# A hybrid Conformer/Hyena block: the second half of the out-projection in a written order

## The chip, the core and the metric

The kernel runs on one core of a Trainium2 chip. The core has TensorE (PE in the profile: matmuls, whose weight loads, PEld, run beside them), VectorE (DVE), ScalarE (ACT), GpSimd (POOL) and SyncE (SP). Each takes its instructions in order from a queue of its own and waits on semaphores for the others. The queues of SP, POOL and ScalarE also issue transfers to 16 shared DMA engines. The metric is the device time of one execution in microseconds: 2048.83 in the median of three runs of the kernel before (2046.94 to 2049.76).

## What is computed

One encoder layer over 2048 positions and 1024 channels, all in float32: a norm, one input projection to 7168 columns, a Conformer branch (GLU, depthwise convolution of width 31, group norm, swish) and a Hyena branch (short convolution, a long convolution by FFT, group RMS norm), each gated, then one output projection, the residual and a last norm. What matters here is the end:

```python
y = bidir_fftconv(v * x1, h_fwd, h_bwd, hy_skip[l]) * x0
y = group_rmsnorm(y, hy_norm_g[l], N_GROUPS_HYENA) * jax.nn.silu(hy_z)
mix = jnp.concatenate([a, y], axis=-1)
h = h + jnp.einsum('blm,md->bld', mix, w_out[l])
return rmsnorm(h, final_g)
```

## The kernel before

The output projection is made in two halves of 1024 rows of `w_out`. The first half, for the Conformer branch, is spread through the FFT as filler (`conf_steps`) and stored to DRAM as `PT`. The second half, for the Hyena branch, is the last stage and the subject here: 16 blocks of 128 positions. To keep float32 precision each operand is split in a high and a low part, so that one product takes three matmuls (`outproj`, L784 to L786). A block has two column halves of 512, each with 8 chunks of k: 16 parts of three matmuls.

A block's operand is made by these steps, whose names are used throughout:

- **Y, T** (`inverted`): the last stage of the inverse FFT (matmul Y from `v`, a tile named long), copies y on ScalarE, transposes T on TensorE, `m<-T,x` on VectorE (times x0), squares sq on ScalarE.
- **gate, m*gate, vp**: gate is SiLU of `hz` on ScalarE, `m<-m,gate` multiplies it in on VectorE, vp is the mean of the squares by TensorE.
- **r, rs** (`deviations`, `stacked`): root on ScalarE, the long reciprocal on VectorE (128x256), two copies on ScalarE, and rs on VectorE.
- **R, m<-R, mh, ml** (`normed`): two pairs of matmuls spread rs over the partitions into R, of which there is one buffer; `m<-m,R` scales m; mh (ScalarE) and ml (VectorE) are the split.

Then (`residual`, `after`) the row of `PT` and the row of x are loaded by POOL and added ("whole", `row<-row,xr`); after each column half VectorE adds the product (`row<-o,row`, the "half add"; two tiles o) and ScalarE squares it with a sum (sqo, ss); behind the second half come sum, root, reciprocal and the scaling of the row (`row<-row,ss,fg`), and SP stores it. SiLU and root lie in different tables of ScalarE, each loaded by an ACT_TABLE_LOAD.

Up to the last parts of the first half the order on TensorE, SP, ScalarE and VectorE is as written (`tc.manual_schedule`). For the 16 blocks themselves it is not: the loop at the end gives, for each b, the steps of block b+2 and then the parts of block b, and the scheduler of the framework puts the instructions of each engine in an order of its own:

```python
*_, (m, vp) = inverted(b + 2, *(rest[2] if b == 0 else fetched(b + 2)))
st[b + 2] = normed(b + 2, m, deviations(vp))
pts[b + 2] = residual(b + 2)
after(b, pts.pop(b), *st.pop(b))
```

Of the kernel before, what the change touches and what calls it, by code (L numbers as in the profile page):

```python
# [11 lines left out]
F32 = mybir.dt.float32  # L12
# [6 lines left out]
P = 128  # L19
# [162 lines left out]
def hybrid_kernel(ctx: ExitStack, tc: tile.TileContext, A, out):  # L182
# [620 lines left out]
    def conf_steps():  # L803


        state[0] = first.pop()
        raw = mixed_load(1, mix[1])
        for i in range(NB):
            parts = state.pop(i)
            pt = row()  # L810
            for group in [(0,), (1,)] if i + 1 < NB else [(0, 1)]:
                if group == (1,):
                    state[i + 1] = mixed(raw, mix[(i + 1) % 2])
                    if i + 2 < NB:
                        raw = mixed_load(i + 2, mix[i % 2])
                o = {c: out_tile() for c in group}
                for k in range(KT):
                    for c in group:
                        outproj(o[c], 0, *parts, HALF[c], k)
                        held[0] += 1  # L820
                        if k + 1 < KT:
                            yield
                for c in group:
                    nc.vector.tensor_copy(pt[:, HALF[c]], o[c])
                    if c == 1:
                        (nc.sync if i < NB - 2 else nc.gpsimd).dma_start(PT[i * P:(i + 1) * P], pt)
                    yield

    conf = conf_steps()
# [107 lines left out]
    with ExitStack() as c0:  # L937
        ep = c0.enter_context(tc.tile_pool(name="ep", bufs=2, reuse_waits="tile"))
        ps = c0.enter_context(tc.tile_pool(name="psE", bufs=1, space=PSUM, reuse_waits="tile"))
        late = []  # L940

        def rows(x, b, cs=slice(0, D)):
# [15 lines left out]
        def opened(hz):  # L958

            gate = ep.tile([P, NG, P], F32, name="gate", bufs=1)  # L960
            nc.scalar.activation(gate, hz, AF.Silu)
            return gate

        def inverted(b, x0, hz, v, gate=None):

            m = ep.tile([P, NG, P], F32, name="m", bufs=3)
            y, sqs = [], []
            for c in range(2):
                Y = ps.tile([P, TC], F32, name="Y", bufs=2)
                for j in range(2):  # L970
                    mm(Y[64 * j:64 * (j + 1)], winv, v[:, j, HALF[c]], start=True, stop=True)  # L971
                y.append(ep.tile([P, TC], F32, name="y"))
                nc.scalar.activation(y[c], Y, AF.Copy)
            yield
            for c in range(2):
                T = ps.tile([P, 4, P], F32, name="T", bufs=2)
                for k in range(4):
                    nc.tensor.transpose(T[:, k], y[c][:, k * P:(k + 1) * P], ident)
                ks = slice(4 * c, 4 * c + 4)
                nc.vector.tensor_mul(m[:, ks], T, x0[:, ks])  # L980
                sq = ep.tile([P, 4, P], F32, name="sq")
                nc.scalar.activation(sq, m[:, ks], AF.Square)
                sqs += [sq[:, :2], sq[:, 2:]]
                yield
            vp = ps.tile([P, 2 * P], F32, name="vp")
            for g, sq in enumerate(sqs):
                mm(vp[32 * g:32 * (g + 1)], ones_g[:, :32], sq, start=True, stop=True)
            nc.vector.tensor_mul(m, m, gate or opened(hz))
            yield m, vp

        def deviations(vp):
            r = ep.tile([P, 2 * P], F32, name="r")
            nc.scalar.activation(r, vp, AF.Sqrt, bias=epst[:, 0:1])
            nc.vector.reciprocal(r, r)
            return r

        def normed(b, m, r):
            rs = ep.tile([P, 2 * P], F32R, name="rs")
            stacked(rs, r)
            mh = late[0].tile([P, NG, P], F32R, name="mh")  # L1000
            ml = late[0].tile([P, NG, P], F32R, name="ml")
            for c in range(2):
                R = ps.tile([P, 4, P], F32, name="R")
                for a in range(2):
                    mm(R[:, 2 * a:2 * a + 2], sel[:, 2 * c + a], rs, start=True, stop=True)
                ks = slice(4 * c, 4 * c + 4)
                nc.vector.tensor_mul(m[:, ks], m[:, ks], R)
                if b < 1:
                    nc.scalar.activation(mh[:, ks], m[:, ks], AF.Copy)
                    nc.vector.tensor_sub(ml[:, ks], m[:, ks], mh[:, ks].bitcast(F32))  # L1010
            if b >= 1:
                nc.scalar.activation(mh, m, AF.Copy)  # L1012
                nc.vector.tensor_sub(ml, m, mh.bitcast(F32))
            return mh, ml

        def residual(b):

            pt = row()
            xr = late[0].tile([P, D], F32, name="xr")
            for (js, src), (_, x) in zip(rows(PT, b), rows(A["x"], b)):  # L1020
                nc.gpsimd.dma_start(pt[js], src)
                nc.gpsimd.dma_start(xr[js], x)
            nc.vector.tensor_add(pt, pt, xr)
            return pt

        def after(b, pt, mh, ml):
            sq = late[0].tile([P, D], F32, name="sqo", bufs=1)
            ss = ep.tile([P, 2], F32, name="ss")
            for c, cs in enumerate(HALF):
                o = out_tile()  # L1030
# [12 lines left out]

        def second(k):
            wo_split(1, k, apad_tile(F32R) if k == 1 else ppad_tile(F32R) if k == 2 else wo_tile(k - 1))

        with tc.manual_schedule(engines={mybir.EngineType.PE, mybir.EngineType.SP,
                                         mybir.EngineType.Activation, mybir.EngineType.DVE}):
            rest = [fetched(b) for b in range(3)]
            gate = opened(rest[0][1])  # L1050
            conf_to(held[0] + 8)
            for k in range(1, 5):
                conf_to(held[0] + 2)
                second(k)
                if k < 3:
                    wo_load(1, k + 5)
            block = inverted(0, *rest[0], gate)
            for _ in range(3):
                next(block)
                conf_to(held[0] + 1)  # L1060
            conf_to(held[0] + 2)
            m, vp = next(block)
            second(5)
            r = deviations(vp)
            second(6)
            for _ in conf:
                pass
            block = inverted(1, *rest[1])
            next(block)
            mctx.close()  # L1070
            late.append(c0.enter_context(tc.tile_pool(name="late", bufs=2, reuse_waits="tile")))
            st = {0: normed(0, m, r)}
            second(7)
            for _ in range(2):
                next(block)
        m, vp = next(block)
        st[1] = normed(1, m, deviations(vp))
        fg = late[0].tile([P, D], F32, name="fg", bufs=1)
        nc.sync.dma_start(fg, bcast(A["final_g"], P))
        pts = {b: residual(b) for b in range(2)}  # L1080
        for b in range(NB):
            if b + 2 < NB:
                *_, (m, vp) = inverted(b + 2, *(rest[2] if b == 0 else fetched(b + 2)))
                st[b + 2] = normed(b + 2, m, deviations(vp))
                pts[b + 2] = residual(b + 2)
            after(b, pts.pop(b), *st.pop(b))


def build(arrays):
# [18 lines left out]
```

## Time and profile before

| | |
|---|---|
| median of three runs | 2048.83 us |
| the profiled execution | 2048.57 us |
| its span | 2046.8 us |
| busy in the span: TensorE, VectorE, ScalarE, GpSimd | 1981.5, 1486.7, 1046.6, 44.2 us |

The span is what the trace covers, from the first instruction to the last; the execution's own time is 1.77 us longer. The chain that ended last is TensorE for 71% of the span. The second half of the out-projection takes about the last 270 us of it. Rows of the timeline give the start and the duration of an instruction in microseconds, and in brackets how long the engine stood idle before it and what ended that. The durations of neighbours on one engine overlap a little, as an instruction starts before the one ahead of it has quite ended.

### The profile page before, as it was taken

The numbers are of one execution on the slowest core, as the hardware profiler recorded it, in microseconds if no ns is written. First come the engines' busy times: TensorE is split into PE (matmuls) and PEld (weight loads), VectorE is DVE, ScalarE is ACT, GpSimd is POOL, SyncE is SP. The second block draws the span as 40 slices with busy tenths as digits, with TensorE's granted clock in tenths as the row PEclk, the third lists the DMA queues.
The fourth block names the chain that finished last, engine by engine and source line by source line (L and its number), as shares of the span: only waits on it lengthen the run. The fifth ranks groups of instructions, "written<-read, shape, count | busy, mean of one in ns | idle before, by whom it ended". The sixth has DMA issues, their size and how long they took to land.

```text
span 2046.8 us, 23642 instructions
## 1 busy us (share of the span) xinstructions
PE 1981.5 (97%) x9304; PEld 1456.5 (71%) x9304; DVE 1486.7 (73%) x1339; ACT 1046.6 (51%) x1410; POOL 44.2 (2%) x90
## 2 busy tenths in 40 slices
PE   6999999999999999999999999999999999989998
PEld 4766688887787887887877877776655555556666
DVE  5587729499599599697795995997455555566774
ACT  5478711253343433433433534445677778555662
POOL 0000000000000000000000000000100000111110
PEclk9999999999999999999999999999999999999999
DMA  8524411120311212113202213121898888997862
GB/s 305 192 98 152 172 37 62 42 82 31 103 52 52 83 62 83 59 45 93 83 23 81 83 31 103 31 83 52 252 282 252 251 263 259 323 246 225 233 171 62
DMA packets 159663, 265.76 MB, mean 130 GB/s; under 512 B 12854, under 2 KB 99254, under 8 KB 155456
## 3 DMA queue, kind: packets, MB, share of 16 engines
q1 hardware_dynamic: 152448, 240.13, 38.0%
q0 software_dynamic: 7104, 24.12, 4.2%
q8 instruction: 73, 1.20, 0.3%
q14 instruction: 38, 0.31, 0.1%
HBM read 163.54 MB, written 100.66 MB: 129 GB/s over the span
## 4 chain that ended last, share of the span: by engine, by line
PE 71%; DVE 18%; issue 6%; ACT 3%; DMA 3%; POOL 0%; SPq 0%; DVEq 0%; POOLq 0%; ACTq 0%
PE mm L246 13%; PE mm L248 13%; PE mm L247 13%; DVE long L541 7%; PE o L784 6%; PE o L785 5%; PE o L786 5%; PE u L874 3%; PE k L874 3%; DVE long L622 2%; DVE long L621 2%; PE aux L679 1%; PE hp L382 1%; PE Y L971 1%; DVE t L622 1%
## 5 line engine op out<-in xcount | busy, mean ns | idle before, releaser
L246 PE MATMUL mm<-uh,wh 128*128 128x512 f32 x1792 | 710.3, 397 | 6.8 <-ACT wh L237 3.5
L248 PE MATMUL mm<-uh,wl 128*128 128x512 f32 x1792 | 702.4, 392 | 4.1 <-DVE wl L239 4.1
L247 PE MATMUL mm<-ul,wh 128*128 128x512 f32 x1792 | 702.3, 392 | 1.7 <-DVE ul L307 1.7
L541 DVE SCALAR_TENSOR_TENSOR long<-apad,small,long 128x2048 f32<-128x2048 f32 x240 | 564.5, 2352 | 8.9 <-ACT long L538 6.9
L246 PEld LDWEIGHTS mm<-uh,wh 128*128 128x128 f32 x1792 | 337.7, 189 | 107.3 <-issue 25.1
L248 PEld LDWEIGHTS mm<-uh,wl 128*128 128x128 f32 x1792 | 338.1, 189 | 78.5 <-DVE wl L239 5.1
L247 PEld LDWEIGHTS mm<-ul,wh 128*128 128x128 f32 x1792 | 338.3, 189 | 76.5 <-DVE ul L307 3.7
L608 ACT ACTIVATE ppad<-mm 128x512 f32<-128x512 f32 x96 | 57.3, 597 | 218.6 <-PE mm L248 196.6
L784 PE MATMUL o<-wo,mh 128*128 128x512 f32 x384 | 155.4, 405 | 1.5 <-ACT mh L1012 1.5
L786 PE MATMUL o<-wo,ml 128*128 128x512 f32 x384 | 152.4, 397 | 0.1
L785 PE MATMUL o<-wo,mh 128*128 128x512 f32 x384 | 152.5, 397 | 0.0
L883 ACT ACTIVATE long<-long 32x1024 f32<-32x1024 f32 x128 | 135.3, 1057 | 2.1
L237 ACT ACTIVATE wh<-wr 128x1024 fp32r<-128x1024 f32 x56 | 59.6, 1064 | 140.1 <-PE mm L247 129.8
L533 DVE TENSOR_TENSOR apad<-mm,apad 128x512 f32<-128x512 f32 x32 | 22.1, 691 | 147.4 <-PE mm L248 147.4
L889 DVE TENSOR_TENSOR long<-long,k 128x1024 f32<-128x1024 f32 x64 | 75.4, 1217 | 72.8 <-PE k L874 67.1
L784 PEld LDWEIGHTS o<-wo,mh 128*128 128x128 f32 x384 | 72.2, 188 | 46.2 <-issue 30.0
L239 DVE TENSOR_TENSOR wl<-wr,wh 128x1024 fp32r<-128x1024 f32 x56 | 68.6, 1225 | 41.7 <-ACT wh L237 41.0
L621 DVE SCALAR_TENSOR_TENSOR long<-ppad,small,long 128x512 f32<-128x512 f32 x64 | 85.8, 1343 | 6.5 <-ACT long L619 6.5
L619 ACT ACTIVATE long<-ppad,small 128x512 f32<-128x512 f32 x64 | 84.7, 1324 | 3.6 <-DMA HZ<-long 1.4
L622 DVE SCALAR_TENSOR_TENSOR long<-ppad,small,long 128x512 f32<-128x512 f32 x64 | 86.4, 1350 | 0.1
L786 PEld LDWEIGHTS o<-wo,ml 128*128 128x128 f32 x384 | 72.4, 189 | 17.5 <-issue 2.5
L785 PEld LDWEIGHTS o<-wo,mh 128*128 128x128 f32 x384 | 72.3, 188 | 17.7 <-issue 4.5
(176 smaller groups left out, 2294.5 us busy)
## 6 DMA issues: line engine op xcount, KB each, us to landing
wr<-in_w_in_dram SPq DMA_DIRECT2D x56, 512.0 KB, 3.6
AK<-ak SPq DMA_DIRECT2D x64, 256.0 KB, 2.0
AU<-t SPq DMA_DIRECT2D x64, 256.0 KB, 3.1
au<-AU SPq DMA_DIRECT2D x64, 256.0 KB, 4.3
ak<-AK SPq DMA_DIRECT2D x64, 256.0 KB, 5.2
VD<-vs SPq DMA_DIRECT2D x64, 256.0 KB, 4.4
long<-VD SPq DMA_DIRECT2D x16, 1024.0 KB, 7.5
xn<-in_x_dram SPq DMA_DIRECT2D x16, 512.0 KB, 5.7
```

What stands on the lines that cost most here:

```text
L246: mm(pt, wh[:, k], uh[t][:, k], start=(k == 0), stop=False)
L247: mm(pt, wh[:, k], ul[t][:, k], start=False, stop=False)
L248: mm(pt, wl[:, k], uh[t][:, k], start=False, stop=(k == KT - 1))
L541: nc.vector.scalar_tensor_tensor(acc, apad[:, j:j + L], sm("dw_w", i * CK + j), acc, op0=OP.mult, op1=OP.add)
L619: nc.scalar.activation(co, v(ppad[:, a + 1:a + 1 + n]), AF.Identity, bias=sm("sh_b", j), scale=sm("sh_w", 3 * j + 1))
L621: nc.vector.scalar_tensor_tensor(co, v(ppad[:, a:a + n]), sm("sh_w", 3 * j), co, op0=OP.mult, op1=OP.add)
L622: nc.vector.scalar_tensor_tensor(co, v(ppad[:, a + 2:a + 2 + n]), sm("sh_w", 3 * j + 2), co, op0=OP.mult, op1=OP.add)
L784: mm(o, mh[:, k], wh[:, cs], start=(k == 0), stop=False)
L785: mm(o, mh[:, k], wl[:, cs], start=False, stop=False)
L786: mm(o, ml[:, k], wh[:, cs], start=False, stop=(k == KT - 1))
L874: mm(o[rows2(k), HALF[i]], g[rows2(i), j:j + 64], x[rows2(i), HALF[k]], start=True, stop=True)
L883: nc.scalar.activation(uw[32 * q:32 * (q + 1)], us[32 * (q ^ 1):32 * (q ^ 1) + 32], AF.Copy)
```

## The change

The loop over the blocks moves into `tc.manual_schedule`, so that its order on TensorE, SP, ScalarE and VectorE is the one written. A block's 16 parts carry a table of hooks, and the steps stand at fixed parts: for blocks 1 to 15 "whole" and rs of the next block at part 2, Y of the block after it at 3, the two R pairs of the next block at 5 and 6, the two T at 7 and 9, the first half add at 10, gate and m*gate at 11, vp, root and long reciprocal at 13; loads of block b+4 at 6. Block 0 has a table of its own. Besides, mh and ml get two pools with one buffer each (`near`), the low parts of two weight pieces are made later, the last two stores of `PT` go by SP, loads are issued two blocks earlier, and of the last block's stores every second one is issued by ScalarE.

```diff
+        def invert(b):
+
+            if b < NB:
+                if b not in B:
+                    B[b] = inverted(b, *rest.pop(b), gate if b == 0 else None)
+                V[b] = next(B[b])
+
+        def deviate(b):
+            if b < NB:
+                r = ep.tile([P, 2 * P], F32, name="r")
+                nc.scalar.activation(r, V[b][1], AF.Sqrt, bias=epst[:, 0:1])
+                nc.vector.reciprocal(r, r)
+                R[b] = r
+
+        def stack(b):
+            if b < NB:
+                rs = ep.tile([P, 2 * P], F32R, name="rs")
+                stacked(rs, R.pop(b))
+                M[b] = normed(b, V.pop(b)[0], rs)
...
+            def whole():
+                nc.vector.tensor_add(pt, pt, xr)
+                residual(b + 2)
+
+            def half(c):
+                cs = HALF[c]
+                nc.vector.tensor_add(pt[:, cs], o[c], pt[:, cs])
+                nc.scalar.activation(sq[:, cs], pt[:, cs], AF.Square, accum_out=ss[:, c:c + 1])
+
+            for c in range(2):
+                o[c] = out_tile()
                 for k in range(KT):
-                    outproj(o, 1, mh, ml, cs, k)
-                nc.vector.tensor_add(pt[:, cs], o, pt[:, cs])
-                nc.scalar.activation(sq[:, cs], pt[:, cs], AF.Square, accum_out=ss[:, c:c + 1])
+                    for f in hooks.get(8 * c + k, ()):
+                        whole() if f == "whole" else half(0) if f == "half" else f()
+                    outproj(o[c], 1, mh, ml, HALF[c], k)
+            half(1)
...
-                for js, dst in rows(out, b, cs):
-                    nc.sync.dma_start(dst, pt[js, cs])
+                for j, (js, dst) in enumerate(rows(out, b, cs)):
+                    (nc.scalar if j and b == NB - 1 else nc.sync).dma_start(dst, pt[js, cs])
...
+                else:
+                    hooks = {2: ["whole", on(stack, b + 1)], 3: [on(invert, b + 2)], 5: [on(scale, b + 1)],
+                             6: [on(scale, b + 1), on(load, b + 4)], 7: [on(invert, b + 2)], 9: [on(invert, b + 2)],
+                             10: ["half"], 11: [on(invert, b + 2)], 13: [on(invert, b + 2), on(deviate, b + 2)]}
+                block(b, hooks)
```

VectorE in one block of the middle, the kernel before, from a long reciprocal on (L994 is the long reciprocal, L1033 a half add, L1023 "whole", L1040 the scaling):

```order
L994 RECIPROCAL r<-r 128x256
L1033 TENSOR_TENSOR row<-o,row 128x512
L229 SCALAR_TENSOR_TENSOR rs<-rs,part,r 128x256
L1007 TENSOR_TENSOR m<-m,R 128x512 x2
L1033 TENSOR_TENSOR row<-o,row 128x512
L1013 TENSOR_TENSOR ml<-m,mh 128x1024
L1023 TENSOR_TENSOR row<-row,xr 128x1024
L1036 TENSOR_TENSOR ss<-ss 128x1
L980 TENSOR_TENSOR m<-T,x_13059 128x512 x2
L1038 RECIPROCAL ss<-ss 128x1
L1040 SCALAR_TENSOR_TENSOR row<-row,ss,fg 128x1024
L988 TENSOR_TENSOR m<-m,gate 128x1024
```

The same engine and length in the changed kernel (L1040 is now the long reciprocal, L1079 a half add, L1074 "whole", L1094 the scaling):

```order
L1040 RECIPROCAL r<-r 128x256
L1079 TENSOR_TENSOR row<-o,row 128x512
L1090 TENSOR_TENSOR ss<-ss 128x1
L1092 RECIPROCAL ss<-ss 128x1
L1094 SCALAR_TENSOR_TENSOR row<-row,ss,fg 128x1024
L1074 TENSOR_TENSOR row<-row,xr 128x1024
L229 SCALAR_TENSOR_TENSOR rs<-rs,part,r 128x256
L1002 TENSOR_TENSOR m<-m,R 128x512 x2
L1008 TENSOR_TENSOR ml<-m,mh 128x1024
L981 TENSOR_TENSOR m<-T,x_13113 128x512 x2
L1079 TENSOR_TENSOR row<-o,row 128x512
L986 TENSOR_TENSOR m<-m,gate 128x1024
```

The instructions of a block are the same ones. Between the long reciprocal and rs stood one half add; now the second half add, the sum, the small reciprocal, the scaling and "whole" stand there. The first half add has moved from there to behind ml and the two products with T.

ScalarE in one block of the middle, the kernel before (L1037 is the root of the row's sum, L993 the root r, L961 the gate):

```order
L1012 ACTIVATE mh<-m 128x1024
L1034 ACTIVATE sqo,ss<-row 128x512
L973 ACTIVATE y<-Y 128x512 x2
L1037 ACT_TABLE_LOAD
L1037 ACTIVATE ss<-ss,epst 128x1
L982 ACTIVATE sq<-m 128x512 x2
L993 ACTIVATE r<-vp,epst 128x256
L961 ACT_TABLE_LOAD
L961 ACTIVATE gate<-hz 128x1024
L227 ACTIVATE rs<-r 128x256
L1034 ACTIVATE sqo,ss<-row 128x512
L228 ACTIVATE r<-r,part 128x256
```

And in the changed kernel (L1091 is the root of the row's sum, L1039 the root r, L962 the gate):

```order
L1007 ACTIVATE mh<-m 128x1024
L983 ACTIVATE sq<-m 128x512 x2
L1080 ACTIVATE sqo,ss<-row 128x512
L962 ACT_TABLE_LOAD
L962 ACTIVATE gate<-hz 128x1024
L1039 ACT_TABLE_LOAD
L1039 ACTIVATE r<-vp,epst 128x256
L1080 ACTIVATE sqo,ss<-row 128x512
L1091 ACTIVATE ss<-ss,epst 128x1
L227 ACTIVATE rs<-r 128x256
L228 ACTIVATE r<-r,part 128x256
L974 ACTIVATE y<-Y 128x512 x2
```

There are two table loads in both. The gate stood behind the root r; it now stands ahead of it, with a table load on either side, and behind the square of the first half add.

## Rows read from the trace of the kernel before

**Rows 1.** Busy time, granted clock (PEclk) and DMA by stretch.

```profile
1862.00:2000.00 138.00, 138.00 (x679) 95.87 (x675) 98.63 (x125) 86.67 (x144) 18.32 (x36) 1.00 0.72 206
```

**Rows 2.** Timeline of TensorE: start, duration, line, operation.

```profile
1775.12 3.37 PE L971 MATMUL Y<-long,winv 128*64 128x512 f32 x8 [2.91 <-DMA long<-VD]
...
1800.41 0.80 PE L1005 MATMUL R<-rs,sel 128*128 128x256 f32 x2 [6.13 <-DVE rs L229]
...
1813.23 0.48 PE L1005 MATMUL R<-rs,sel 128*128 128x256 f32 x2
...
1830.92 0.63 PE L987 MATMUL vp<-sq,ones_g 128*32 128x256 f32 x4
...
1850.71 0.62 PE L987 MATMUL vp<-sq,ones_g 128*32 128x256 f32 x4 [2.48 <-ACT sq L982]
...
1922.12 0.51 PE L1005 MATMUL R<-rs,sel 128*128 128x256 f32 x2
...
1923.71 1.94 PE L971 MATMUL Y<-long,winv 128*64 128x512 f32 x8
...
2012.39 0.40 PE L1005 MATMUL R<-rs,sel 128*128 128x256 f32 x2
```

**Rows 3.** Timeline of VectorE at the start of the stage.

```profile
1769.97 1.75 DVE L994 RECIPROCAL r<-r 128x256 f32<-128x256 f32 x1 [0.57 <-ACT r L993]
1771.64 1.31 DVE L491 SCALAR_TENSOR_TENSOR wo<-t,small,wo 128x512 fp32r<-128x512 f32 x2
...
1795.40 1.23 DVE L1023 TENSOR_TENSOR row<-row,xr 128x1024 f32<-128x1024 f32 x1 [7.65 <-issue]
```

**Rows 4.** Timeline of the end, behind the last matmul.

```profile
2038.66 0.69 DVE L1033 TENSOR_TENSOR row<-o,row 128x512 f32<-128x512 f32 x1 [4.82 <-PE o L786]
...
2040.86 1.42 DVE L1040 SCALAR_TENSOR_TENSOR row<-row,ss,fg 128x512 f32<-128x512 f32 x2
2041.64 2.38 SPq L1042 DMA_DIRECT2D out_dram<-row  x4
```

**Rows 5.** Timeline of VectorE in one block of the middle.

```profile
1921.38 0.69 DVE L1007 TENSOR_TENSOR m<-m,R 128x512 f32<-128x512 f32 x1 [1.29 <-PE R L1005]
1922.67 0.69 DVE L1007 TENSOR_TENSOR m<-m,R 128x512 f32<-128x512 f32 x1 [0.60 <-PE R L1005]
1923.82 0.69 DVE L1033 TENSOR_TENSOR row<-o,row 128x512 f32<-128x512 f32 x1 [0.46 <-PE o L786]
...
1926.21 1.23 DVE L1023 TENSOR_TENSOR row<-row,xr 128x1024 f32<-128x1024 f32 x1 [0.31 <-DMA row<-PT]
1927.35 0.15 DVE L1036 TENSOR_TENSOR ss<-ss 128x1 f32<-128x1 f32 x1
1927.42 1.28 DVE L980 TENSOR_TENSOR m<-T,x 128x512 f32<-128x512 f32 x2
...
1928.81 1.28 DVE L1040 SCALAR_TENSOR_TENSOR row<-row,ss,fg 128x1024 f32<-128x1024 f32 x1
1930.01 1.22 DVE L988 TENSOR_TENSOR m<-m,gate 128x1024 f32<-128x1024 f32 x1
...
1934.99 0.48 DVE L229 SCALAR_TENSOR_TENSOR rs<-rs,part,r 128x256 fp32r<-128x256 f32 x1 [1.24 <-ACT r L228]
```

**Rows 6.** Timeline of ScalarE in the same block.

```profile
1923.59 1.06 ACT L1012 ACTIVATE mh<-m 128x1024 fp32r<-128x1024 f32 x1 [4.02 <-PE o L785]
1924.55 0.63 ACT L1034 ACTIVATE sqo<-row 128x512 f32<-128x512 f32 x1
1925.08 0.19 ACT L1034 ACTIVATION_READ_ACCUMULATOR sqo<-row 128x1 f32 x1
...
1930.36 0.47 ACT L993 ACTIVATE r<-vp,epst 128x256 f32<-128x256 f32 x1 [0.99 <-PE vp L987]
1930.85 1.28 ACT L961 ACT_TABLE_LOAD   x1
1932.14 1.06 ACT L961 ACTIVATE gate<-hz 128x1024 f32<-128x1024 f32 x1
```

More of the change, by code (lines that the diff above doesn't have):

```diff
@@ L939, in hybrid_kernel @@
         ps = c0.enter_context(tc.tile_pool(name="psE", bufs=1, space=PSUM, reuse_waits="tile"))
+        near = [c0.enter_context(tc.tile_pool(name="near0", bufs=1, reuse_waits="tile"))]
         late = []
@@ L984, in inverted @@
                 yield
+            nc.vector.tensor_mul(m, m, gate or opened(hz))
+            yield
             vp = ps.tile([P, 2 * P], F32, name="vp")
@@ L987, in inverted, with normed @@
                 mm(vp[32 * g:32 * (g + 1)], ones_g[:, :32], sq, start=True, stop=True)
-            nc.vector.tensor_mul(m, m, gate or opened(hz))
             yield m, vp
[L991 to L1001, printed above, removed]
+        def normed(b, m, rs):
+            mh = near[b % 2].tile([P, NG, P], F32R, name="mh")
+            ml = near[b % 2].tile([P, NG, P], F32R, name="ml")
             for c in range(2):
@@ L1007, in normed @@
                 nc.vector.tensor_mul(m[:, ks], m[:, ks], R)
-                if b < 1:
+                if b == 0:
                     nc.scalar.activation(mh[:, ks], m[:, ks], AF.Copy)
                     nc.vector.tensor_sub(ml[:, ks], m[:, ks], mh[:, ks].bitcast(F32))
[L1011 to L1014, printed above, removed]
-        def residual(b):
[L1018 to L1024, printed above, removed]
@@ L1026, in after, with second, low @@
-        def after(b, pt, mh, ml):
+                elif c:
+                    nc.scalar.activation(mh, m, AF.Copy)
+                    nc.vector.tensor_sub(ml, m, mh.bitcast(F32))
+                yield mh, ml
+        def second(k):
+            tile = apad_tile(F32R) if k == 1 else ppad_tile(F32R) if k == 2 else wo_tile(k - 1)
+            wh, wl = wo[1, k] = tile[:, :D], tile[:, D:2 * D]
+            g = sm("hn_g", k)
+            raw = [wo_raw.pop((1, k, c)) for c in range(2)]
+            for c, cs in enumerate(HALF):
+                nc.scalar.activation(wh[:, cs], raw[c], AF.Copy, scale=g)
+            def low():
+                for c, cs in enumerate(HALF):
+                    nc.vector.scalar_tensor_tensor(wl[:, cs], raw[c], g, wh[:, cs].bitcast(F32),
+                                                   op0=OP.mult, op1=OP.subtract)
+            return low
@@ new lines, in scale, with load, block @@
+        def scale(b):
+            if b < NB:
+                H[b] = next(M[b])
+        def residual(b):
+            if b < NB:
+                X[b] = row(), late[0].tile([P, D], F32, name="xr")
+                for to, src in zip(X[b][::-1], (A["x"], PT)):
+                    for js, r in rows(src, b):
+                        nc.gpsimd.dma_start(to[js], r)
+        def load(b):
+            if b < NB:
+                rest[b] = fetched(b)
+        def block(b, hooks):
+            mh, ml = H.pop(b)
+            pt, xr = X.pop(b)
@@ L1027, in after @@
             sq = late[0].tile([P, D], F32, name="sqo", bufs=1)
             ss = ep.tile([P, 2], F32, name="ss")
-            for c, cs in enumerate(HALF):
-                o = out_tile()
+            o = [None, None]
+            def whole():
[5 more added lines that the diff above has]
+                nc.scalar.activation(sq[:, cs], pt[:, cs], AF.Square, accum_out=ss[:, c:c + 1])
@@ L1040, in after, with on @@
                 nc.vector.scalar_tensor_tensor(pt[:, cs], pt[:, cs], s, fg[:, cs], op0=OP.mult, op1=OP.mult)
-                for js, dst in rows(out, b, cs):
-                    nc.sync.dma_start(dst, pt[js, cs])
-        def second(k):
-            wo_split(1, k, apad_tile(F32R) if k == 1 else ppad_tile(F32R) if k == 2 else wo_tile(k - 1))
+                for j, (js, dst) in enumerate(rows(out, b, cs)):
+                    (nc.scalar if j and b == NB - 1 else nc.sync).dma_start(dst, pt[js, cs])
+        def on(f, *args):
+            return lambda: f(*args)
         with tc.manual_schedule(engines={mybir.EngineType.PE, mybir.EngineType.SP,
                                          mybir.EngineType.Activation, mybir.EngineType.DVE}):
-            rest = [fetched(b) for b in range(3)]
+            rest = {b: fetched(b) for b in range(3)}
             gate = opened(rest[0][1])
@@ L1053, in hybrid_kernel @@
                 conf_to(held[0] + 2)
-                second(k)
+                second(k)()
                 if k < 3:
                     wo_load(1, k + 5)
-            block = inverted(0, *rest[0], gate)
             for _ in range(3):
-                next(block)
+                invert(0)
                 conf_to(held[0] + 1)
[L1061 to L1065, printed above, removed]
+            invert(0)
@@ L1066, in hybrid_kernel @@
+            conf_to(held[0] + 1)
+            invert(0)
+            second(5)()
+            deviate(0)
+            low = second(6)
             for _ in conf:
                 pass
-            block = inverted(1, *rest[1])
-            next(block)
+            load(3)
+            stack(0)
+            invert(1)
+            scale(0)
+            invert(1)
             mctx.close()
+            near.append(c0.enter_context(tc.tile_pool(name="near1", bufs=1, reuse_waits="tile")))
             late.append(c0.enter_context(tc.tile_pool(name="late", bufs=2, reuse_waits="tile")))
-            st = {0: normed(0, m, r)}
@@ L1073, in hybrid_kernel @@
[L1073 to L1086, printed above, removed]
+            fg = late[0].tile([P, D], F32, name="fg", bufs=1)
@@ new lines, in hybrid_kernel @@
+            for b in range(2):
+                residual(b)
+            scale(0)
+            invert(1)
+            low()
+            low = second(7)
+            for b in range(NB):
+                if b == 0:
+                    hooks = {1: [low, on(invert, 1)], 3: [on(invert, 1), on(deviate, 1)], 4: [on(invert, 2)],
+                             6: [on(nc.sync.dma_start, fg, bcast(A["final_g"], P)), on(load, 4)], 7: [on(invert, 2)], 8: [on(invert, 2)], 9: [on(stack, 1)],
+                             11: [on(scale, 1), on(invert, 2)], 12: [on(scale, 1)],
+                             13: [on(invert, 2), on(deviate, 2)], 14: ["whole"], 15: ["half"]}
+                else:
[3 more added lines that the diff above has]
+                block(b, hooks)
```

3 lines of the change are left out of this document (2 added, 1 removed).

## The prediction

> **What bounds the kernel now.** I read the granted clock and busy time by stretch first, then TensorE's timeline, then VectorE's and ScalarE's over one block. From 1862 to 2000 us TensorE is busy the whole stretch at full clock [rows 1]; nothing done on VectorE or ScalarE there can make it faster. Losses lie before: 6.13 us where the broadcast R waits for VectorE's rs, 2.91 us at Y, 2.48 us at vp, and slow stretches right behind the first two [rows 2]. VectorE shows why R waited: the add of the residual stood in its queue ahead of rs and ran only at 1795.40 after 7.65 us of idling for its data [rows 3]. So two things can be gained (the first blocks, and the end) and one can be lost (the rhythm of the middle). The marks I count by are the R pairs: that of block 2 starts at 1813.23, that of block 15 at 2012.39 [rows 2]; between them lie 13 blocks, 199.2 us, 15.32 each. From R of block 15 to the end of the last matmul (about 2038.63, where the last half add starts [rows 4]) are 26.2 us, and the span ends 8.2 us later at 2046.8.
>
> **The middle: one circle per block.** TensorE's work per block is the same: 48 matmuls of out-projection, one Y, two T, one vp, two R. What changes is the order on VectorE and ScalarE, which is now the order in which they run. Following it, the rs of one block depends on the rs of the block before through engine queues alone, and that circle can be added up. I take each step from its start to the start of the next, for VectorE with the overlap that the rows show:
>
> - rs 0.48 and 0.05 until R starts (the delay from m<-R's end at 1922.07 to R at 1922.12); R to m<-R 0.55 (1922.12 to 1922.67): 1.08 [rows 2, 5].
> - First to second m<-R, with R's second pair between since there is one R buffer: 1.29 (1921.38 to 1922.67) [rows 5].
> - Second m<-R 0.69, hand-over 0.04, mh 1.06, hand-over 0.02: 1.81 [rows 5, 6].
> - ml, which now stands ahead of the two m<-T: 1.14, the step of the 1024-wide add at 1926.21; the two m<-T 1.28 less an overlap of 0.08: 1.20 [rows 5].
> - The first half add, now behind them, with hand-over 0.73 (1923.82 to 1924.55), its square with the read of the sum 0.74: 1.47 [rows 5, 6].
> - ScalarE then has, behind that square, the table load 1.29, gate 1.06 and 0.02, a second table load 1.30, the root r 0.47 and 0.03: 4.17 [rows 6].
> - The long reciprocal 1.67 (1769.97 to 1771.64), which now stands ahead of the second half add [rows 3].
> - From the second half add to the scaling of the row, through square, sum, root and reciprocal: 2.20 (2038.66 to 2040.86) [rows 4].
> - Scaling 1.20 (1928.81 to 1930.01), and the residual add "whole" of the next block 1.14, both now ahead of rs [rows 5].
>
> Sum: 1.08 + 1.29 + 1.81 + 1.14 + 1.20 + 1.47 + 4.17 + 1.67 + 2.20 + 2.34 = 18.4 us per block, against 15.3 of TensorE's work. So TensorE, in order too, must wait at each R for rs: about 2.7 us, since R's second pair also follows one part (0.69) behind the first and not about 0.94, and waits some 0.3 for m<-R. In the kernel before, the gate was made a block ahead (m*gate runs at 1930.01, the gate after it only at 1932.14 [rows 5, 6]), so no table load stood between a half's square and the long reciprocal, and rs did not stand behind scaling and "whole"; the same instructions then fit under TensorE. VectorE's instructions are as many as before and ScalarE still loads its table twice a block: it is not work that grows but the length of the path. 13 circles are 239.4 us; less 199.2, **+40.2 us**. Bounds: if hand-overs or overlaps let it fall below TensorE's work, 15.7 a block (15.3 and the R wait) is the floor, +4.9; each 0.1 us of error in the circle is 1.3 us.
>
> On the table loads: root r starts 1930.36, ends 1930.83, the load starts 1930.85 and gate 1.29 later at 1932.14, so nothing but its 1.28 us shows [rows 6]. The Trainium skill (ScalarE: Activation LUTs, What ACT_TABLE_LOAD costs) counts besides the load a drain of 1.38 us for every change of table; by it, as an estimate, two per circle would give 21.1 us a block and 2110 us in all. The rows do not show that drain, so the sum goes by 1.28.
>
> **The start.** The reciprocal at 1769.97 stays [rows 3]. Behind it come now the two copies of the last first-half tile (1.2 us; the two low halves, 1.31, move behind), rs at 1772.8, R 1773.4, m<-R 1773.9, mh and ml by halves (0.63, 0.69). So block 0 can start near 1776.0. Then the second m<-R and m<-T end at 1779.2, square 1779.9, vp; ScalarE needs 1.3 for two weight pieces, table 1.3, gate 1.1, table 1.3, root 0.5: 1785.3; reciprocal to 1787.0; y, m<-T and squares of block 2 and the copies for rs of block 1 take to 1790.4, R of block 1. Gate of block 2 holds VectorE until 1792.2, m*gate 1793.4, second m<-R 1794.1, mh 1795.1, table and root 1796.9, reciprocal 1798.5, whole 1799.8, first half add 1800.5. Block 1 needs that half add, since there are two out tiles: TensorE waits about 4.9 us for it, starts block 1 at 1800.5, and after five parts (3.45) and Y (2.06) R of block 2 starts at 1806.1. Before it was 1813.23: **-7.2 us**. Smaller waits of block 0 (0.4 to 1.8 us) are in that count. I take -7.2; from -10 (the 4.9 us halved) to 0 (data late again).
>
> The moved transfers cost nothing by this: whole of block 0 is asked for at 1798.5, and before the data was there at 1795.40 with the last PT store behind another 1.31 us on VectorE. That store on SP holds the loads of block 3 behind it until about 1773; they are wanted at Y of block 3, near 1802. In the middle a load is issued two blocks before its use, and at 18.4 us a block the 3.5 MB a block ask for less than the 206 GB/s of before [rows 1].
>
> **The end.** R of block 15 now lies at part 5 of block 14: 11 parts (7.6), the R pairs and their wait (0.9), and block 15 (11.1) follow, 0.2 to the last one's end: 19.8 us where it was 26.2, since R of block 15 stood among block 13's last parts before: **-6.4**. The last stores go half by ScalarE's queue: the four took SP 2.38 us [rows 4], so one issue of 0.6 less: **-0.6** (from -1.1 to 0).
>
> Sum: +40.2 - 7.2 - 6.4 - 0.6 = +26.0 on the profiled execution's own 2048.57 (span 2046.8 and 1.77 around it), which is within 0.3 of the median 2048.83: **2074.6 us**.
>
> **Rivals.**
> - *The circle is shorter than TensorE's work, so the kernel is faster.* Place: rs in VectorE's queue; it decides when the circle is under 16.4 us, where the loss is eaten by the other three terms. Then 13 x 15.7 gives +4.9, and 4.9 - 7.2 - 6.4 - 0.6 = -9.3: 2039. For it: TensorE was saturated with these same instructions. Against: two whole microseconds of the sum would have to be wrong, and each of its steps is a row.
> - *The waits throttle TensorE.* Behind 2.91 us of waiting, Y took 3.37 us where it takes 1.94, and behind 6.13 us an R pair 0.80 where it takes 0.51; behind 2.48 us vp took 0.62 as without a wait (0.63) [rows 2]. That is 1.2 GHz in place of 2.4. My wait of 2.7 lies between. With both R at the lower level the circle grows by 0.57, with T late too by up to 1.43: 13 times that, 2082 to 2093. The Trainium skill (TensorE: Matmul & The Clock Gate, HAM oscillation) describes such a loop, in which each wait sends the array back to the low clock; the trace agrees for the two longer waits. A slower array also fills the wait, which works against it.
> - *The start's data is late.* If PT lands late, whole of block 0, and so block 1, slides one for one; 6 us more than I have is 2081.
>
> **How the numbers follow.** Circle at full clock 0.66 (2074.6, own range 2066 to 2082); throttled 0.15 (2082 to 2093); late start 0.05 (2081); faster 0.10 (about 2039); in between, about as long as before, 0.04. The first carries the predicted time. From 2058 to 2092 some 0.83 is held: what is left out is the faster case, the middle one and a rest at the top. Within 0.2% is 4 us, what a measurement of this kernel can tell from no change: faster 0.10, same 0.04, slower 0.86.
>
> **What would show it.** R of block 2 near 1806, then R pairs 18.4 us apart with TensorE idle 2 to 3 us ahead of each, released by rs on VectorE; ScalarE with square, load, gate, load, root in one row without a gap; VectorE with long reciprocal, second half add and scaling in one row behind them; the last R near 2045. Wrong would be R pairs 15 to 16 us apart, a wait at R that ends by anything but rs, or waits for DMA in the middle.

## The result and the profile after

The changed kernel takes 2083.74 us in the median of four runs (2077.1 to 2088.3), against 2048.57 for the kernel before (four runs, 2046.94 to 2049.76): a ratio of 1.017, interval 1.014 to 1.020. It is slower by 35 us, where 26 were forecast. The execution with the profile is the longest of the four, 2088.3 us, with a span of 2086.5.

The waits of TensorE in the last stage come first (engine, operation and line, what was waited for: sum in us, times, longest):

```profile
PE o L784 <- DVE row L1079: 4.9, 1, 4.9
PE R L1000 <- DVE rs L229: 32.2, 15, 4.0
```

Fifteen waits for rs, one ahead of the first R pair of every block but block 2, make up nearly all of it. The next rows are the stretch of [rows 1], then two neighbouring blocks in it from R pair to R pair, and then 3.5 us of each, from 0.8 us behind its R on (busy time and instructions of TensorE, its weight loads, VectorE, ScalarE and GpSimd, granted clock, DMA share, GB/s):

```profile
1862.00:2000.00 138.00, 120.21 (x555) 80.56 (x553) 83.05 (x105) 72.52 (x120) 14.26 (x28) 0.96 0.77 190
1887.58:1906.79 19.21, 17.25 (x77) 11.80 (x77) 11.16 (x14) 9.92 (x16) 2.04 (x5) 0.91 0.78 192
1906.79:1925.12 18.33, 15.78 (x76) 10.60 (x77) 11.06 (x14) 9.88 (x16) 2.03 (x5) 1.00 0.81 200
1888.40:1891.90 3.50, 3.43 (x12) 2.67 (x11) 1.49 (x3) 1.06 (x1) 1.02 (x2) 0.53 0.92 257
1907.60:1911.10 3.50, 3.42 (x19) 2.57 (x18) 1.79 (x3) 1.06 (x1) 0.99 (x2) 1.00 1.01 259
```

TensorE, busy all 138 us before [rows 1], is now busy 120.2, at a mean clock of 0.96. The first three blocks after R of block 2 are 18.28, 19.06 and 19.23 us long; from R of block 5 on two lengths alternate, 18.3 and 19.2 us. The longer one has a stretch at a clock of 0.53 shortly behind its R, about the lower of the two levels; the shorter one stays at 1.00. TensorE's timeline at the marks of [rows 2] (start, duration, and in brackets the idle time before and what ended it):

```profile
1804.42 0.77 PE L784 MATMUL o<-wo,mh 128*128 128x512 f32 x1 [4.93 <-DVE row L1079]
...
1887.58 0.48 PE L1000 MATMUL R<-rs,sel 128*128 128x256 f32 x2 [2.48 <-DVE rs L229]
1888.84 0.80 PE L1000 MATMUL R<-rs,sel 128*128 128x256 f32 x2
...
1906.79 0.47 PE L1000 MATMUL R<-rs,sel 128*128 128x256 f32 x2 [1.89 <-DVE rs L229]
1908.04 0.50 PE L1000 MATMUL R<-rs,sel 128*128 128x256 f32 x2
...
2057.00 0.77 PE L1000 MATMUL R<-rs,sel 128*128 128x256 f32 x2 [3.97 <-DVE rs L229]
```

Behind the wait of 2.48 us at 1887.58 the first R pair still takes its usual time and the second 0.80 in place of 0.50; behind the wait of 1.89 both are quick. Two earlier blocks belong beside them: block 4 slows down in the same way behind a wait of 2.16, and block 3, behind 2.48, is slow from its first R pair on (0.76). R of block 2 starts at 1812.66 and that of block 15 at 2057.00: 244.3 us for the 13 blocks that took 199.2 before, 18.80 each.

VectorE in a quick block of the middle, where [rows 5] show it before:

```profile
1906.16 0.48 DVE L229 SCALAR_TENSOR_TENSOR rs<-rs,part,r 128x256 fp32r<-128x256 f32 x1
...
1908.57 0.69 DVE L1002 TENSOR_TENSOR m<-m,R 128x512 f32<-128x512 f32 x1 [0.59 <-PE R L1000]
1910.39 1.23 DVE L1008 TENSOR_TENSOR ml<-m,mh 128x1024 fp32r<-128x1024 f32 x1 [1.12 <-ACT mh L1007]
1911.53 1.28 DVE L981 TENSOR_TENSOR m<-T,x 128x512 f32<-128x512 f32 x2
1912.73 0.68 DVE L1079 TENSOR_TENSOR row<-o,row 128x512 f32<-128x512 f32 x1
1916.57 1.23 DVE L986 TENSOR_TENSOR m<-m,gate 128x1024 f32<-128x1024 f32 x1 [3.16 <-ACT gate L962]
1918.36 1.75 DVE L1040 RECIPROCAL r<-r 128x256 f32<-128x256 f32 x1 [0.56 <-ACT r L1039]
1920.03 0.63 DVE L1079 TENSOR_TENSOR row<-o,row 128x512 f32<-128x512 f32 x1
...
1922.16 1.28 DVE L1094 SCALAR_TENSOR_TENSOR row<-row,ss,fg 128x1024 f32<-128x1024 f32 x1
1923.37 1.22 DVE L1074 TENSOR_TENSOR row<-row,xr 128x1024 f32<-128x1024 f32 x1
1924.50 0.48 DVE L229 SCALAR_TENSOR_TENSOR rs<-rs,part,r 128x256 fp32r<-128x256 f32 x1
```

And ScalarE in the same block, for [rows 6]:

```profile
1913.44 0.63 ACT L1080 ACTIVATE sqo<-row 128x512 f32<-128x512 f32 x1
1913.98 0.19 ACT L1080 ACTIVATION_READ_ACCUMULATOR sqo<-row 128x1 f32 x1
1914.18 1.28 ACT L962 ACT_TABLE_LOAD   x1
1915.48 1.06 ACT L962 ACTIVATE gate<-hz 128x1024 f32<-128x1024 f32 x1
1916.56 1.28 ACT L1039 ACT_TABLE_LOAD   x1
1917.85 0.47 ACT L1039 ACTIVATE r<-vp,epst 128x256 f32<-128x256 f32 x1
1920.69 0.63 ACT L1080 ACTIVATE sqo<-row 128x512 f32<-128x512 f32 x1 [2.36 <-DVE row L1079]
```

Read down both columns in order of time and the whole block is one line, from rs at 1906.16 to rs at 1924.50: the half add at 1912.73 ends just as ScalarE is done with the squares sq, the square of the row follows both, this square stands ahead of load, gate, load and root on ScalarE without a gap, the root releases the reciprocal at 1918.36, and behind it on VectorE stand the second half add (1920.03), the sum and the small reciprocal, the scaling, "whole", and only then rs at 1924.50. VectorE idles 3.16 us for the gate and ScalarE 2.36 us for the second half add, each for the other, in every such block. Neither is short of time (11.1 and 9.9 us of work in 18.3): it is the path through both that is too long.

The start of the stage, for [rows 3], on VectorE:

```profile
1773.76 1.75 DVE L1040 RECIPROCAL r<-r 128x256 f32<-128x256 f32 x1 [0.47 <-ACT r L1039]
...
1802.39 1.16 DVE L1074 TENSOR_TENSOR row<-row,xr 128x1024 f32<-128x1024 f32 x1
1803.59 1.29 DVE L1079 TENSOR_TENSOR row<-o,row 128x512 f32<-128x512 f32 x2
```

"Whole" no longer waits for anything, where VectorE idled 7.65 us ahead of it before. That it was data it waited for is a reading: the row of [rows 3] names no releaser. It fits, since the loads of these rows left POOL from 1785.74 on and loads of this kind took 7.9 to 11.3 us to land there. The end, for [rows 4], on VectorE and on the queues of SP and ScalarE:

```profile
2078.96 0.69 DVE L1079 TENSOR_TENSOR row<-o,row 128x512 f32<-128x512 f32 x1 [4.82 <-PE o L786]
...
2081.16 1.42 DVE L1094 SCALAR_TENSOR_TENSOR row<-row,ss,fg 128x512 f32<-128x512 f32 x2
```

```profile
2081.94 1.13 SPq L1096 DMA_DIRECT2D out_dram<-row  x2
2081.94 1.38 ACTq L1096 DMA_DIRECT2D out_dram<-row  x2
```

Two stores on each of two queues take 1.13 and 1.38 us where four on one took 2.38.

This execution reached the stage later than that of before: the long reciprocal of block 0 stands at 1773.76, against 1769.97 [rows 3]. In the kernels below, which share everything up to there, the same instruction stands between 1766 and 1771, so that is a difference between executions. I therefore also give for each kernel the time from this reciprocal to the end of the last matmul: 268.7 us before, 305.2 after.

### The profile page after: what moved, and what is told of

Same layout as the page of the kernel before. It is cut to its first block, busy times and chain, and to the rows that moved or that the text cites. A ratio compares the mean times of both kernels' runs of the same rounds, so it can differ in the third digit from the quotient of the medians.

```text
span 2086.5 us, 23595 instructions
## 1 busy us (share of the span) xinstructions
PE 1994.4 (96%) x9304; PEld 1466.2 (70%) x9304; DVE 1487.7 (71%) x1339; ACT 1049.4 (50%) x1410; POOL 43.1 (2%) x88
## 4 chain that ended last, share of the span: by engine, by line
PE 65%; DVE 20%; ACT 7%; issue 6%; DMA 2%; SPq 0%; DVEq 0%; POOL 0%; ACTq 0%; POOLq 0%
PE mm L246 13%; PE mm L248 13%; PE mm L247 13%; DVE long L541 7%; PE o L784 4%; PE o L785 3%; PE o L786 3%; PE u L874 3%; PE k L874 2%; DVE long L622 2%; DVE long L621 2%; PE aux L679 1%; DVE r L1040 1%; PE hp L382 1%; ACT L1039 1%
## 5 line engine op out<-in xcount | busy, mean ns | idle before, releaser
L784 PE MATMUL o<-wo,mh 128*128 128x512 f32 x384 | 163.3, 425 | 4.9 <-DVE row L1079 4.9
L785 PE MATMUL o<-wo,mh 128*128 128x512 f32 x384 | 154.3, 402 | 0.0
L784 PEld LDWEIGHTS o<-wo,mh 128*128 128x128 f32 x384 | 75.0, 195 | 56.1 <-issue 44.0
L785 PEld LDWEIGHTS o<-wo,mh 128*128 128x128 f32 x384 | 75.2, 196 | 12.1
```

The source lines that it names most:

```text
L784: mm(o, mh[:, k], wh[:, cs], start=(k == 0), stop=False)
L785: mm(o, mh[:, k], wl[:, cs], start=False, stop=False)
```

## The experiments

My theory: the block is bound by the circle of queue steps through VectorE and ScalarE, 18.35 us at full clock, and the waits that it makes cost another 0.9 us in every second block through the clock. Rivals: the clock does most of it, the circle only part; the table loads do it, by more than their 1.28 us; the moved transfers do it; or a written order as such is worse than the scheduler's. The ratios below go by the kernel before as it was measured again beside these kernels: 2048.44 us in the median for the first four, 2048.12 for the last three.

**The gate ahead of the squares.** SiLU, with its table load, is written at Y (part 3) for blocks 3 to 15, in place of part 11; m*gate stays:

```diff
             m = ep.tile([P, NG, P], F32, name="m", bufs=3)
             y, sqs = [], []
+            if b >= 3:
+                gate = opened(hz)
```

> The changed kernel, but for blocks 3 to 15 the SiLU for the gate is written ahead of Y (part 3) instead of behind the square of the first half add (part 11); the number of table loads is the same. Theory (a circle of queue steps through VectorE and ScalarE, 18.4 us a block, sets the pace): one table load and the gate (1.29 + 1.08 us) leave the circle, R pairs come 16.0 us apart, TensorE waits 0.3 us at R, and with waits that short its clock stays up: about 2045 us (2040 to 2052). Rival A (TensorE's own written order, or transfers, set the pace): R pairs stay 18.4 to 19.2 apart, 2077 to 2088. Rival B (the two table loads a block cost what they cost wherever they stand): no gain, above 2075.

Measured: 2044.96 us (2042.38 to 2047.51), ratio to before 0.999, interval 0.998 to 1.000; 266.4 us from the reciprocal to the last matmul. ScalarE in a block of the middle:

```profile
1901.64 1.28 ACT L962 ACT_TABLE_LOAD   x1
1902.93 1.06 ACT L962 ACTIVATE gate<-hz 128x1024 f32<-128x1024 f32 x1
...
1910.64 0.63 ACT L1082 ACTIVATE sqo<-row 128x512 f32<-128x512 f32 x1
1911.17 0.19 ACT L1082 ACTIVATION_READ_ACCUMULATOR sqo<-row 128x1 f32 x1
1911.38 1.28 ACT L1041 ACT_TABLE_LOAD   x1
1912.67 0.47 ACT L1041 ACTIVATE r<-vp,epst 128x256 f32<-128x256 f32 x1
```

There are still two loads in a block. One of them, with the gate, has only gone from between square and root to a place where ScalarE was waiting. R pairs come 15.98 us apart, the trace lists no wait for rs in the middle, and the clock is 1.00. So the place of this one step is worth 38.8 us, more than the whole loss. Load and gate, 2.34 us, are off the path, and 18.35 less 2.34 is the 16.0 that is seen. The 38.8 us also hold what the clock had cost in the middle, since the waits behind which it fell are gone.

**rs ahead of "whole".** The two hooks of part 2 exchanged:

```diff
-                    hooks = {2: ["whole", on(stack, b + 1)], ...
+                    hooks = {2: [on(stack, b + 1), "whole"], ...
```

> The changed kernel, but at part 2 the copies and rs of the next block are written ahead of the residual add whole instead of behind it. Theory of the circle: whole (1.14 us) leaves the path to rs, but then stands in front of later work; worked through the queues the circle is 17.7 to 17.8 us, TensorE waits about 1.6 at rs and 0.8 at the second R pair, 13 blocks give 9 us, and some of the throttled stretches go: 2066 to 2076. Rival A (TensorE's order or transfers): no change, 2077 to 2088.

Measured: 2067.2 us (2064.59 to 2068.57), ratio 1.0097, interval 1.0082 to 1.0113; 290.4 us from the reciprocal. R pairs come 17.61 us apart, each behind a wait of about 1.37 for rs and 0.47 for m<-R:

```profile
1909.63 0.48 DVE L229 SCALAR_TENSOR_TENSOR rs<-rs,part,r 128x256 fp32r<-128x256 f32 x1
1910.02 1.22 DVE L1074 TENSOR_TENSOR row<-row,xr 128x1024 f32<-128x1024 f32 x1
1911.16 0.68 DVE L1002 TENSOR_TENSOR m<-m,R 128x512 f32<-128x512 f32 x1
```

"Whole" has left the path ahead of rs (1.14), but now the first m<-R stands behind it: it starts 0.91 us behind R (1910.25 to 1911.16) where it took 0.51, 0.40 more. The circle falls by 0.74 (1.14 less 0.40), less than the step that was moved: an instruction taken off one link of a queue stands on the next one. Three of the 13 blocks are 18.6 long; in the first of them the mean clock is 0.91, so here too it falls now and then.

**Both.** The two edits together:

> Both edits in one: SiLU ahead of Y, and rs ahead of whole. Theory: the circle falls below TensorE's own work; the R pairs come 15.7 us apart (15.4 and 0.35 of waiting for the single R buffer), no wait at rs remains in the middle: about 2040 us (2035 to 2046), faster than the kernel before. Rival A: 2077 to 2088. Rival C (transfers become the bound once TensorE runs at 15.7 a block): R pairs 16 to 17 apart with waits that end by DMA.

Measured: 2039.39 us (2036.3 to 2040.48), ratio 0.9961, interval 0.9945 to 0.9976; 260.5 us from the reciprocal, R pairs 15.60 apart and without a wait (TensorE's timeline):

```profile
1902.66 0.39 PE L1002 MATMUL R<-rs,sel 128*128 128x256 f32 x2
...
1918.25 0.39 PE L1002 MATMUL R<-rs,sel 128*128 128x256 f32 x2
```

That is near the 15.7 that the prediction gave as the floor for a circle under TensorE's work, and the time is what that rival had for its price, 2039. With two steps moved, the written order beats the scheduler's.

**The waits filled with idle matmuls.** Eleven matmuls with zero weights are added to o in blocks 2 to 14, just ahead of the first R pair of the next block; they change no result and do no useful work:

```diff
+                    if 2 <= b < NB - 1 and 8 * c + k == 5:
+                        for _ in range(11):
+                            mm(o[c], zero, wo[1, k][0][:, HALF[c]], start=False, stop=False)
```

> The changed kernel, but in blocks 2 to 14 eleven matmuls of 128x512 with a weight tile of zeros stand in front of the first R pair, added onto the tile in work (they add nothing to its value): TensorE works 2.5 us where it waited 1.9 to 2.7. Theory (the circle sets 18.35 us; the blocks of 19.2 are those that ran partly at the lower clock behind the wait): with TensorE busy the clock stays full, every block takes 18.35 to 18.5, the middle loses 5 to 6 us and the whole falls to 2074 to 2079 although 143 matmuls are added. Rival (the 19.2 is a step of the circle itself, in turn): R pairs still 18.35 and 19.2 apart, same time. Rival A (TensorE's own work sets the pace): 2.5 us more per block, about 2115.

Measured: 2075.81 us (2075.34 to 2081.21), ratio to before 1.015, interval 1.013 to 1.017; 297.2 us from the reciprocal, 8.0 less than after. The four runs overlap with those of the changed kernel (2077.1 to 2088.3), so the case rests on the traces. Rows of TensorE and of VectorE, and one block as a window:

```profile
1895.62 2.70 PE L1091 MATMUL o<-wo,zero 128*128 128x512 f32 x11
1898.29 0.48 PE L1004 MATMUL R<-rs,sel 128*128 128x256 f32 x2
```

```profile
1897.67 0.48 DVE L233 SCALAR_TENSOR_TENSOR rs<-rs,part,r 128x256 fp32r<-128x256 f32 x1
```

```profile
1879.94:1898.29 18.35, 18.27 (x88) 12.67 (x88) 11.06 (x14) 9.89 (x16) 2.03 (x5) 1.00 0.81 201
```

No wait for rs shows any more but in the last block (1.98), because TensorE is busy where it waited, yet every block is 18.35 us long. TensorE is now busy for 18.27 us of each, so its row alone does not tell what sets the pace. VectorE's does: rs ends at 1898.15, 0.14 us ahead of R, as it did in the quick blocks of the changed kernel (1906.64 and 1906.79), where TensorE had 1.89 us to spare. It is still the circle. The clock is 1.00 from R of block 2 to that of block 15, and the 19.2 us blocks are gone. This splits the loss in the middle: 3.0 us a block is the circle, 0.45 in the mean (0.86 in every second one) the clock. The clock doing most of it is ruled out. Of the 8.0 us, 5.8 lie in the 13 blocks, and 1.1 in the end. The other 1.1 lies ahead of the first added matmul and is no effect of them: from the reciprocal to R of block 2 the profiled execution of the changed kernel took 38.9 us, the six kernels of this section that keep its written start, this one among them, 37.8 to 38.4.

**The scheduler for the blocks again.** Start, buffers, stores and loads of the changed kernel, and its order of the code, but the loop over the blocks outside `tc.manual_schedule`:

```diff
-            for b in range(NB):
+        for b in range(NB):
```

> The changed kernel with its written start, but the loop over the 16 blocks (hooks, pools and early loads as changed) stands outside the written order, so that the scheduler orders its instructions again. Theory: the start keeps its gain and the middle goes back to 15.3 to 15.6 a block, since the loss lies in the written order of VectorE and ScalarE alone: 2036 to 2046 us. Rival (the pools of one buffer for mh and ml, or the earlier loads, lengthen the block): R pairs over 17 us apart, above 2065.

Measured: 2046.79 us (2043.91 to 2050.4), ratio 0.9996, interval 0.9985 to 1.0008; 269.1 us from the reciprocal. This just misses what was expected. The later blocks are as thought, R pairs 15.25 to 15.9 apart from block 5 to block 14. But the scheduler's first blocks give the start away again (VectorE's timeline):

```profile
1830.51 1.23 DVE L1074 TENSOR_TENSOR row<-row,xr 128x1024 f32<-128x1024 f32 x1 [10.76 <-DMA row<-PT]
...
1831.72 0.48 DVE L229 SCALAR_TENSOR_TENSOR rs<-rs,part,r 128x256 fp32r<-128x256 f32 x1
```

"Whole" is put ahead of rs of block 3 while its row is still under way, VectorE idles 10.76 us, and R waits 8.63: the same fault as [rows 3] show at block 1. So the buffers and the earlier loads cost the middle next to nothing. The scheduler's order of the middle is short because it makes the gate a block ahead, as before (m*gate at 1935.11, the gate behind it at 1936.36). What it does not find is an order that keeps late data from standing ahead of rs.

**An order by the path.** Most steps on the circle are written earlier: "whole" behind rs and Y at part 3, the first R pair and both T at 5, SiLU at 7, the half add at 8, m*gate at 9, vp, root and reciprocal at 10:

```diff
-                    hooks = {2: ["whole", on(stack, b + 1)], 3: [on(invert, b + 2)], 5: [on(scale, b + 1)],
-                             6: [on(scale, b + 1), on(load, b + 4)], 7: [on(invert, b + 2)], 9: [on(invert, b + 2)],
-                             10: ["half"], 11: [on(invert, b + 2)], 13: [on(invert, b + 2), on(deviate, b + 2)]}
+                    hooks = {3: [on(stack, b + 1), on(invert, b + 2), "whole"],
+                             5: [on(scale, b + 1), on(invert, b + 2), on(invert, b + 2)],
+                             6: [on(scale, b + 1), on(load, b + 4)], 7: [on(silu, b + 2)], 8: ["half"],
+                             9: [on(invert, b + 2)], 10: [on(invert, b + 2), on(deviate, b + 2)]}
```

> The changed kernel with another written order for blocks 1 to 15, worked out on the circle: rs of the next block, then Y and whole at part 3, first R pair and both T at 5, second R pair at 6, SiLU at 7, first half add at 8, m*gate at 9, vp, root and long reciprocal at 10. Theory: the circle lies under TensorE's work also with hand-overs of 0.1 us, the second R pair finds m<-R done: R pairs 15.35 apart, no waits in the middle: 2032 to 2040 us, 3 to 6 us less than with the two edits alone. Rival C (transfers become the bound): waits that end by DMA in the middle, 2040 or more.

Measured: 2032.67 us (2031.65 to 2035.46), ratio 0.9927, interval 0.9911 to 0.9944; 255.0 us from the reciprocal. R pairs come 15.22 us apart, and the stretch of [rows 1] is full again:

```profile
1862.00:2000.00 138.00, 138.00 (x691) 98.45 (x690) 99.01 (x127) 89.82 (x147) 18.32 (x36) 1.00 0.85 215
```

This is the best version of the study, 15.5 us under the kernel before and 51 under the changed one, with the same instructions. From the reciprocal it is 13.7 us shorter than before: 5.4 up to R of block 2, 2.1 in the 13 blocks and 6.2 behind R of block 15, where the forecast had -7.2 and -6.4 for start and end and a middle that could only lose. Even the stretch that was full before had a little left in it: its steady blocks were 15.39 us long and are 15.22 here, with TensorE shown busy for 138.00 of 138 us both times. The 4.95 us that block 1 waits for block 0's half add is still there in every written order.

**No table loads.** The gate of blocks 3 to 15 is a plain copy, so the two loads of a block go. This kernel leaves SiLU out there, so its output is not the layer's:

```diff
-            nc.vector.tensor_mul(m, m, gate or opened(hz))
+            nc.vector.tensor_mul(m, m, gate or opened(hz, AF.Copy if b >= 3 else AF.Silu))
```

> The changed kernel in its written order, but for blocks 3 to 15 the gate is a plain copy in place of SiLU, which leaves SiLU out of the output there and needs no change of table: both table loads of a block are gone and nothing else moves. Theory: 2.6 us leave the circle, R pairs 15.8 apart, waits short enough for the full clock: 2040 to 2050 us, as much as the move of load and gate gave. Rival (TensorE's order): 2077 to 2088. If a load cost a drain besides its 1.28 us, the circle would lose 5.3 and the block would sit at TensorE's 15.7.

Measured: 2047.39 us (2045.97 to 2050.08), ratio 0.9998, interval 0.9988 to 1.0007; 270.2 us from the reciprocal. R pairs come 16.27 apart, where 15.8 was expected. VectorE shows what took over:

```profile
1911.62 1.23 DVE L986 TENSOR_TENSOR m<-m,gate 128x1024 f32<-128x1024 f32 x1 [1.74 <-ACT gate L962]
1912.76 1.75 DVE L1040 RECIPROCAL r<-r 128x256 f32<-128x256 f32 x1
```

The root is ready at 1911.94 already, but m*gate, which waited for the gate, stands ahead of the reciprocal until 1912.76. So the circle falls by 2.08 and not by the 2.6 of two loads. ScalarE's own rows tell what a load costs there: from the start of the row's square to the end of the root it takes 4.88 us in the changed kernel (1913.44 to 1918.32) and 2.03 here (1909.91 to 1911.94). Of these 2.85 us the two loads are 2.56; most of the other 0.3 is that neighbours without a load between them overlap a little. Nor are the loads the cause as an amount of work: moving one of them, with the gate, brought the block down by 2.4 us (18.35 to 15.98), deleting both by 2.1.

## Why the prediction came out as it did

The direction, the range and the mechanism of the middle were right; the sum was too low, by 9 us against the median. The median lies 1.7 us above the range of the case that was held most likely (2066 to 2082, at 0.66) and inside that of the throttled one, which had 0.15. In the profiled run the stretch from the long reciprocal to the last matmul was forecast at 36.1 + 239.4 + 19.8 = 295.3 us and is 305.2.

- *The circle.* Forecast 18.4 us; at full clock it is 18.35 in the changed kernel's quick blocks and in every block of the filled one. The steps are those of the sum, in its order, each within 0.07 us of its term in the quick block from 1906.16 on, and the releasers (gate, root, half add, rs) those that it names. The moved edits confirm it link by link: 2.4 us less for load and gate, 0.74 for "whole" with m<-R behind it. Two slips in the working did no harm. The ten terms add up to 18.37, and 13 of that are 238.8, not 239.4. And in the kernel before a table load did stand between the half add's square and the long reciprocal (at 1926.31, for the root of the row's sum); behind it ScalarE still waited 0.99 us for vp [rows 6], so it was not on the path.
- *The clock.* This is the term that was mis-sized: the likeliest case set it to nothing and gave the throttled case 0.15. The clock does fall, in seven of the 13 blocks, for some 3 us, and turns 18.35 into 19.21. 13 blocks took 244.3 us in place of 239.4, +4.9: the clock's part is 5.8, by the 238.5 that the filled kernel takes for them, and the circle itself came out 0.9 under the 239.4. The two cases were not the alternatives that I took them for: a wait of 2.48 us was followed by the fall, and the block that follows a slow one waits 0.59 less (1.89), since TensorE's slower work (17.25 in place of 15.78 us) fills the wait while the circle grows by less (0.86). That one ran at full clock, and the next waited 2.48 again. The throttled rival's band, 2082 to 2093, holds the result, although its mechanism is present in about half the blocks only.
- *The start.* Forecast: block 1 begins 30.5 us behind the long reciprocal, after a wait of 4.9. Measured: 30.66 and 4.93. From there to R of block 2 I had 5.6 us and it took 8.24, at a mean clock of 0.66 behind that wait: +2.6, with the clock again. The other kernels with this written start took 7.1 to 7.7 there, so about 1 us of the 2.6 belongs to this execution. The place was right, the rate at which TensorE runs behind a wait was not. The data was in time, so the late-start rival is out.
- *The end.* Forecast 19.8 us from R of block 15 to the last matmul's end, measured 21.9. The first 3.5 us of it are at a clock of 0.50, behind the 3.97 us wait. The kernel with both edits and the one ordered by the path, whose last R waits 1.1 to 1.2 us for rs and then runs at its usual rate, take 20.06.
- *The tail.* From the last matmul to the span's end 7.6 us, 8.2 before: -0.6, as forecast.
- *The table loads.* 1.28 us each with gaps of 0.02 at most around them: the sum by 1.28 gives the 18.35 that is seen, and the 2110 us of the prediction's other reckoning did not come.

The three terms with the clock in them are 4.9, 2.6 and 2.1 us, 9.6 of the 9.9 that the stretch is over its forecast. Another 3.8 us of the profiled execution's 2088.3 is its later arrival at the stage. The clock is a measured cause in the middle (the filled kernel takes it away there); at the start and the end it is read from the windows and was not tried by itself. The four runs agree with it: mean clocks of 0.990, 0.988, 0.986 and 0.985 go with 2077.1, 2082.6, 2084.9 and 2088.3 us.

What stays open: what makes the clock fall. In the changed kernel it fell behind 2.48 and 2.16 us of waiting and not behind 1.89. In the kernel before it did not fall behind the 2.48 us at vp [rows 2]: the 9.3 us from there on are at 1.00. In the filled one it did behind 1.98 us ahead of the last R (0.52 in the next 3.5 us). In the kernel with rs ahead of "whole" two to four blocks with waits of 1.37 and 0.47 pass at full clock and the next one is slow. The length of one wait alone does not decide it. Nor was the 4.9 us at block 1 taken away, since "whole" and the half add of block 0 would have to stand ahead of work of block 2 there.

## What to carry to other kernels

With engines that run in order, look for the circle: follow one step of a block through every queue back to the same step of the next block, and add the starts. If that sum is over the bottleneck engine's work per block, the order is wrong however little the other engines are busy; the cure is to take one slow step (here a gate with its table load) off the path into a gap, and to see which instruction of the queue comes to stand on the path in its place. And price every wait on TensorE twice, once for itself and once for the slower matmuls that may follow it: here 2.5 us of waiting cost up to 0.9 us more.

## What was not expected of the hardware

- Matmuls that do nothing made the 13 blocks of the changed kernel shorter: eleven with zero weights per block, 2.7 us of added TensorE work, took 5.8 us off them by holding the clock at 1.00.
- A kernel can swing between two lengths of block by itself: 18.35 and 19.21 us in turn over its last ten, with waits of 1.89 and 2.48. Some of its buffers alternate from block to block, but they do so in the filled kernel too, where every block is 18.35 long; what alternates is the clock.
